# Moving the transfers of an S5 branch from SyncE's queue to GpSimd's

## The chip, the cores and the metric

The kernel runs on one core of a Trainium2 chip. The time is the device time of one execution in microseconds (us), as the median of several executions. The core has five engines that run their own instruction streams in order: TensorE (PE, with its weight loads shown as PEld), VectorE (DVE), ScalarE (ACT), GpSimd (POOL) and SyncE (SP). Any of the last three can issue DMA transfers, and all transfers are carried by the same 16 DMA engines. In this kernel SyncE issues nearly all of them.

## The reference

The model is a trunk of two layers on 272 tokens (16 meta tokens and 256 inputs) of width 2048, in float32. The first (even) layer is where the change lies. From one input projection it takes queries, keys and values for a grouped attention, and a stream u of width 512 for a bidirectional S5 branch: 32 groups of 16 channels, each with a diagonal complex state of 64, one recurrence per direction. Both results are joined, projected, and followed by a squared-ReLU MLP; the second (odd) layer and its MLP come after and are not touched.

```
def s5_direction(u, lam_re, lam_im, log_dt, b_re, b_im, c_re, c_im):
    ...                     # abar = exp(lam * dt), bbar = (abar - 1) / lam * b, complex
    bu_re = jnp.einsum('blgh,gph->blgp', u, bbar_re)
    bu_im = jnp.einsum('blgh,gph->blgp', u, bbar_im)
    ...
    _, _, x_re, x_im = lax.associative_scan(_complex_scan_combine, (a_re, a_im, bu_re, bu_im), axis=1)
    return jnp.einsum('blgp,ghp->blgh', x_re, c_re) - jnp.einsum('blgp,ghp->blgh', x_im, c_im)

def s5_mixer(u, ...):
    y_fw = s5_direction(uf, ...)
    y_bw = flip_t(s5_direction(flip_t(uf), ...))
    y = y_fw + y_bw + d_skip.astype(f32) * uf
    y = jax.nn.gelu(y.reshape(b, l, S5_WIDTH))
    return y * jax.nn.sigmoid(y @ glu_w.astype(f32) + glu_b.astype(f32))

def even_mixer(h, ...):
    q, k, v, u = jnp.split(h @ w_in, ...)
    ...
    att = grid_attention(q, k, v.reshape(b, l, ATT_KV_HEADS, HEAD_DIM))
    ssm = s5_mixer(u, ...)
    return jnp.concatenate([att.astype(jnp.float32), ssm], axis=-1).astype(h.dtype) @ w_out
```

## The kernel before

All large projections go through one helper, `stream` (from L140). It reads a weight matrix in chunks of mostly 512 KB: each chunk is loaded into a tile `raw` by a DMA on SyncE (L176), split by ScalarE into a rounded high half `wh` (L133) and by VectorE into the rest `wl` (L134), and used by TensorE in three matmuls per block (L166): high by high, high by low, low by high. `raw`, `wh` and `wl` have four buffers each, so a load waits until an older chunk has been split. The activations are split the same way into `xh` and `xl` (L136, L137).

The even layer runs two programs woven into one another in the text. The main one (`even_in`) streams the weights of u first, then ten chunks of q, k and v columns with the attention behind each group of heads, then (`out_a`) the first part of the output projection. The side program is the S5 branch (`S5.run`, then `S5.tail`). It doesn't scan token by token. Tokens are cut into 34 blocks of 8: matrices that hold powers of abar carry a block's inputs to its end state, a scan of 34 steps runs over the blocks, and more matrices bring the states back to the tokens. Groups are handled in eight batches of four:

- `evac_u` (L717) scales the projected u into a tile `up` and stores it to a scratch in DRAM, `s_u` (L724, 4 transfers); `finish_u` (L726) reads it back rearranged into the tile `U` (L731, 8 transfers; each has 16 partitions with 32 runs of 136 bytes). Clearing the edge of the state array EE, which lies in the buffer h, is a GpSimd operation (L927).
- `batch` (L810) loads the b and c coefficients of four groups, `bc` (L815), builds on VectorE the tables W and CA (L734 is the line of the helper through which all these tensor operations go), transposes W (L856) into WT, multiplies CA by bb (L867), stores CA to a DRAM scratch `s_ca` (L870), and assembles from the product a tile `Kf` of 16 partitions. Eight transfers (L880) copy shifted windows of Kf, four runs of 512 bytes in each of 16 partitions, into the 128 partitions of the matrix `M`. CA, Kf, M, W and WT have one buffer each, bc has two.
- `apply` (L885) multiplies WT and M by U (`pe`, L893, and `pm`, L902).
- After the last batch two transfers (L928, L929) swap the halves of EE (shown as h<-h), and the scan runs on VectorE (L931 on). `tail` reloads CA (L959), applies it (L963, L964), and moves the result through DRAM once more (L976, L978) before the gate `glu`.

GpSimd has little else in this layer: four loads of constants at the start, and clears of edge regions of `V`, `qr` and `sq` for the attention (L641, L578).

The order of the work on each engine is not written by hand. A planner goes through the program with a model of each engine's time, and takes what is ready by priority: the place in the text, moved ahead by 50 for the split and load of weights, by 500 for `URGENT` pieces such as `apply` and the scan, and by 0 for a batch's tables. Each engine then runs its list in order, and each wait at the head of a list holds what stands behind.

Of the kernel before, what the change touches and what calls it, by code (L numbers as in the profile page):

```python
# [15 lines left out]
P = 128  # L16
# [687 lines left out]
class S5:  # L704
# [12 lines left out]
    def evac_u(self, ft):  # L717
        nc = self.nc
        acc = self.T.h[:, ft]
        up = self.p2.tile([P, S5C, S5J], F32, name="up", tag="sg")  # L720
        nc.vector.tensor_tensor(out=up.rearrange("p s j -> p j s"),
                                in0=acc.rearrange("p (j s) -> p j s", s=S5C),
                                in1=self.T.rb.rearrange("p (j s) -> p j s", s=S5C), op=ALU.mult)
        nc.sync.dma_start(out=self.ud[ft * P:(ft + 1) * P], in_=up)  # L724

    def finish_u(self):  # L726
        nc = self.nc
        self.U = self.p1.tile([P, S5G, S5J], F32, name="U")
        v = self.ud.rearrange("(g h) s j -> s h g j", h=16)
        for s in range(S5C):  # L730
            nc.sync.dma_start(out=self.U[s * 16:(s + 1) * 16], in_=v[s])  # L731

    def tt(self, out, a, b, op):
        self.nc.vector.tensor_tensor(out=out, in0=a, in1=b, op=op)  # L734
# [75 lines left out]
    def batch(self, b):  # L810
        nc, I, p1, p2, tt, T = self.nc, self.I, self.p1, self.p2, self.tt, self.T
        mul, add, sub = ALU.mult, ALU.add, ALU.subtract
        g0 = b * NB
        bc = p2.tile([P, 4, 2, NB, 16], F32, name="bc")
        nc.sync.dma_start(out=bc, in_=I["s5_bc"][:, b])  # L815
        bb = p1.tile([P, 2, 2, NB, 16], F32, name="bb")
        nc.vector.tensor_scalar_mul(out=bc[:, 2:], in0=bc[:, 2:], scalar1=self.sg[:, 1:2])
        btmp = p1.tile([P, 2, NB, 16], F32, name="btmp")

        def gsel(x):  # L820
            return x.rearrange("p (d g) -> p d g", d=2)[:, :, g0:g0 + NB].unsqueeze(3).broadcast_to([P, 2, NB, 16])

        cr, ci = gsel(self.cr), gsel(self.ci)
        tt(bb[:, 0], bc[:, 0], cr, mul)
        tt(btmp, bc[:, 1], ci, mul)
        tt(bb[:, 0], bb[:, 0], btmp, add)
        tt(bb[:, 1], bc[:, 1], cr, mul)
        tt(btmp, bc[:, 0], ci, mul)
        tt(bb[:, 1], bb[:, 1], btmp, sub)
        yield  # L830

        def table(dst, tmp, Pa, Pb, A, B, d, lo, n, rev):
            ks = slice(lo, lo + n)

            def pw(x):
                v = x[:, ks, d * S5G + g0:d * S5G + g0 + NB]
                if rev:
                    v = v[:, ::-1]
                return v.rearrange("p k g -> p g k").unsqueeze(3).broadcast_to([P, NB, n, 16])

            def cf(x):
                return x.unsqueeze(2).broadcast_to([P, NB, n, 16])

            tt(dst, pw(Pa), cf(A), mul)
            tt(tmp, pw(Pb), cf(B), mul)
            tt(dst, dst, tmp, add)

        W = p1.tile([P, 2, NB, S5C, 16], F32, name="W")
        wt = p1.tile([P, NB, 9, 16], F32, name="wtmp")
        WT = p1.tile([P, 2, NB, P], F32, name="WT")  # L850
        for d in range(2):
            table(W[:, d], wt[:, :, :S5C], self.P1, self.P2, bb[:, 0, d], bb[:, 1, d], d, 0, S5C, d == 0)
            with T.tc.high_priority(offset=URGENT):
                pt = T.mx([P, NB, P], "wtp")
                for g in range(NB):
                    nc.tensor.transpose(pt[:, g], W[:, d, g].rearrange("p s h -> p (s h)"), T.ident)  # L856
                nc.scalar.copy(out=WT[:, d], in_=pt)
            yield
        CA = p1.tile([P, 2, NB, 9, 16], F32, name="CA")
        kp = []  # L860
        for d in range(2):
            table(CA[:, d], wt, self.P1, self.P2, bc[:, 2, d], bc[:, 3, d], d, 0, 9, d == 1)
            with T.tc.high_priority(offset=URGENT):
                ps = T.mx([16, NB, P], "kps")
                for g in range(NB):
                    lo = 0 if d == 0 else 1
                    nc.tensor.matmul(ps[:, g], bb[:, 0, d, g], CA[:, d, g, lo:lo + 8], start=True, stop=True)  # L867
            kp.append(ps.rearrange("p g (t h) -> p g t h", h=16))
            yield
        nc.sync.dma_start(out=self.cad[b], in_=CA.rearrange("p d g t h -> p (d g t h)"))  # L870
        Kf = p1.tile([16, NB, 15, 16], F32, name="Kf")
        nc.scalar.copy(out=Kf[:, :, 8:15], in_=kp[0][:, :, 1:8])
        nc.scalar.copy(out=Kf[:, :, 0:8], in_=kp[1])
        tt(Kf[:, :, 7], kp[0][:, :, 0], Kf[:, :, 7], add)
        dm = p1.tile([16, NB, 16], F32, name="dm")
        tt(dm, self.drow[:, g0:g0 + NB], T.ident[:16, :16].unsqueeze(1).broadcast_to([16, NB, 16]), mul)
        tt(Kf[:, :, 7], Kf[:, :, 7], dm, add)
        M = p1.tile([P, NB, P], F32, name="M")
        for s in range(S5C):
            nc.sync.dma_start(out=M[s * 16:(s + 1) * 16].rearrange("p g (t h) -> p g t h", h=16),  # L880
                                in_=Kf[:, :, 7 - s:15 - s])
        yield
        self.batches.append((b, WT, M))
# [22 lines left out]
    def run(self):  # L906
        nc, T, p1, p2, tt = self.nc, self.T, self.p1, self.p2, self.tt
        mul, add = ALU.mult, ALU.add
        self.batches = []
        yield from self.base()  # L910
        for b in range(S5G // NB):
            bt = self.batch(b)
            while True:
                with T.tc.high_priority(offset=0):
                    if next(bt, 0) == 0:
                        break
                yield
            while not hasattr(self, "U"):
                yield
            ap = self.apply(*self.batches.pop())  # L920
            while True:
                with T.tc.high_priority(offset=URGENT):
                    if next(ap, 0) == 0:
                        break
                yield
        EE = self.EE
        nc.gpsimd.memset(EE[:, :, 0], 0.0)  # L927
        nc.sync.dma_start(out=EE[64:, 1, 1:], in_=EE[:64, 0, 1:])  # L928
        nc.sync.dma_start(out=EE[:64, 1, 1:], in_=EE[64:, 0, 1:])  # L929
        yield  # L930
        for j in range(1, S5J - 1):  # L931
            with T.tc.high_priority(offset=URGENT):
                t1 = p2.tile([P, 2, 64], F32, name="z1")
                t2 = p2.tile([P, 2, 64], F32, name="z2")
                x = EE[:, :, j]
                tt(t1, self.PP[:, 0], x, mul)
                tt(t2, self.PP[:, 1], x[:, ::-1], mul)
                tt(t1, t1, EE[:, :, j + 1], add)
                tt(EE[:, :, j + 1], t1, t2, add)
            if j % 4 == 0:  # L940
                yield
# [454 lines left out]
```

## Time and profile before

| | us |
|---|---|
| median of three runs | 2409.11 (2406.84 to 2411.78) |
| profiled execution | 2411.23 |
| its span, first to last instruction | 2409.3 |
| TensorE busy | 2348.9 (97%) |
| VectorE busy | 1441.7 (60%) |
| ScalarE busy | 1132.0 (47%) |
| GpSimd busy | 64.4 (3%) |

Mean granted TensorE clock is 0.989 of full speed. A profile row gives the engine, the line of the kernel, the operation, the tile it writes and what it reads; `[2.59 <-DVE wl L134]` at the end of a row says that the engine was idle for 2.59 us just before, and which operation ended that. SPq is SyncE's queue, whose rows are the issues of transfers; when the data landed is told in a view of its own. A matmul's duration overlaps that of the next one, so the rate is read from counts, not durations.

### The profile page before, as it was taken

How to read it: one execution, taken by the hardware profiler on the slowest of the kernel's cores; microseconds unless marked ns; L12 is line 12 of the kernel's file. 1: busy time of each engine (PE TensorE's matmuls, PEld its weight loads, DVE VectorE, ACT ScalarE, POOL GpSimd, SP SyncE). 2: the span in 40 equal slices, each digit the busy share in tenths (PEclk: the TensorE clock that was granted, in tenths of full speed). 3: DMA queues.
4: the chain of work that ended last, by engine and by line, in shares of the span. 5: the costliest groups of instructions: out<-in, count | busy, mean ns of one | idle time of the engine just before them, and what ended most of it. 6: DMA issues, size and time to landing. Idle time of an engine off the chain costs nothing.

```text
span 2409.3 us, 42429 instructions
## 1 busy us (share of the span) xinstructions
PE 2348.9 (97%) x17287; PEld 2243.4 (93%) x17287; DVE 1441.7 (60%) x2351; ACT 1132.0 (47%) x1754; POOL 64.4 (3%) x116
## 2 busy tenths in 40 slices
PE   7999999999999999999989999999999999999998
PEld 7889899999999999999989999999988988988987
DVE  8786837654554454555679667656644544555555
ACT  5566734543443343344456434444544443443443
POOL 0000001100000000000110000001000000000000
PEclk9999999999999999999999999999999999999999
DMA  7545464555555555555452543564555555555554
GB/s 265 167 146 174 125 199 141 166 172 176 171 181 176 176 169 182 170 180 183 161 174 83 167 149 125 189 198 146 183 185 190 185 176 189 187 186 192 184 186 146
DMA packets 131458, 415.49 MB, mean 172 GB/s; under 512 B 23504, under 2 KB 30048, under 8 KB 130496
## 3 DMA queue, kind: packets, MB, share of 16 engines
q1 hardware_dynamic: 130816, 412.35, 53.7%
q8 instruction: 135, 2.21, 0.4%
q14 instruction: 59, 0.48, 0.1%
q0 software_dynamic: 160, 0.35, 0.1%
q10 hardware_dynamic: 288, 0.10, 0.0%
HBM read 401.62 MB, written 7.95 MB: 170 GB/s over the span
## 4 chain that ended last, share of the span: by engine, by line
PE 89%; DVE 4%; ACT 2%; POOL 1%; issue 1%; DMA 0%; DVEq 0%; SPq 0%; ACTq 0%; POOLq 0%
PE acc L166 81%; POOL h L293 1%; DVE wl L134 1%; PE po L690 1%; DVE res L290 1%; DVE xl L137 1%; PE mo L1180 1%; PE pe L893 1%; PE kps L867 1%; PE sc L667 1%; PE ro L1256 1%; ACT wh L133 0%; PE ptp L683 0%; PE pc L219 0%; PE rs L1247 0%
## 5 line engine op out<-in xcount | busy, mean ns | idle before, releaser
L134 DVE TENSOR_TENSOR wl<-raw,wh 128x1024 fp32r<-128x1024 f32 (+1 forms) x730 | 890.2, 1220 | 840.1 <-ACT wh L133 836.4
L133 ACT CAST wh<-raw 128x1024 fp32r<-128x1024 f32 (+1 forms) x730 | 757.9, 1039 | 1013.1 <-PE acc L166 968.1
L166 PE MATMUL acc<-xh,wh 128*128 128x272 f32 (+1 forms) x3728 | 1070.8, 288 | 25.4 <-ACT wh L133 9.7
L166 PE MATMUL acc<-xl,wh 128*128 128x272 f32 (+1 forms) x3728 | 1073.1, 288 | 5.5 <-DVE xl L137 5.1
L166 PE MATMUL acc<-xh,wl 128*128 128x272 f32 (+1 forms) x3728 | 1070.9, 288 | 6.5 <-DVE wl L134 6.5
L166 PEld LDWEIGHTS acc<-xh,wh 128*128 128x128 f32 x3728 | 707.3, 190 | 28.9 <-ACT wh L133 9.8
L166 PEld LDWEIGHTS acc<-xl,wh 128*128 128x128 f32 x3728 | 709.4, 190 | 9.2 <-DVE xl L137 7.8
L166 PEld LDWEIGHTS acc<-xh,wl 128*128 128x128 f32 x3728 | 707.6, 190 | 9.3 <-DVE wl L134 7.6
L166 PE MATMUL acc<-h1l,wh 128*128 128x272 f32 x1024 | 295.8, 289 | 0.0
L166 PE MATMUL acc<-h1h,wl 128*128 128x272 f32 x1024 | 295.2, 288 | 0.0
L166 PE MATMUL acc<-h1h,wh 128*128 128x272 f32 x1024 | 293.8, 287 | 0.0
L166 PE MATMUL acc<-wh,h1l 128*128 128x512 f32 (+1 forms) x528 | 204.8, 388 | 0.0
L166 PE MATMUL acc<-wh,h1h 128*128 128x512 f32 (+1 forms) x528 | 204.7, 388 | 0.0
L166 PE MATMUL acc<-wl,h1h 128*128 128x512 f32 (+1 forms) x528 | 203.9, 386 | 0.0
L166 PEld LDWEIGHTS acc<-h1h,wh 128*128 128x128 f32 x1024 | 193.0, 188 | 0.0
L166 PEld LDWEIGHTS acc<-h1l,wh 128*128 128x128 f32 x1024 | 192.7, 188 | 0.0
L166 PEld LDWEIGHTS acc<-h1h,wl 128*128 128x128 f32 x1024 | 192.4, 188 | 0.0
L166 PEld LDWEIGHTS acc<-wh,h1l 128*128 128x128 f32 x528 | 99.2, 188 | 21.8
L166 PEld LDWEIGHTS acc<-wl,h1h 128*128 128x128 f32 x528 | 99.3, 188 | 21.6
L166 PEld LDWEIGHTS acc<-wh,h1h 128*128 128x128 f32 x528 | 99.4, 188 | 21.1
L293 POOL TENSOR_TENSOR h<-h,res 128x272 f32<-128x272 f32 (+1 forms) x42 | 47.8, 1152 | 576.0 <-DVE res L290 576.0
L368 ACT ACTIVATE relu<-acc 128x272 f32<-128x272 f32 (+1 forms) x128 | 48.3, 391 | 27.5 <-PE acc L166 27.5
(319 smaller groups left out, 1492.9 us busy)
## 6 DMA issues: line engine op xcount, KB each, us to landing
raw<-in_w SPq DMA_DIRECT2D x504, 512.0 KB, 3.5
raw<-in_w_odd SPq DMA_DIRECT2D x88, 512.0 KB, 3.4
raw<-in_w_even SPq DMA_DIRECT2D x40, 512.0 KB, 4.4
raw<-in_wo_odd SPq DMA_DIRECT2D x24, 512.0 KB, 3.9
raw<-in_wo_a SPq DMA_DIRECT2D x24, 384.0 KB, 3.9
s_ca<-CA SPq DMA_DIRECT2D x8, 576.0 KB, 3.6
CA<-s_ca SPq DMA_DIRECT2D x8, 576.0 KB, 4.8
h<-in_hT SPq DMA_DIRECT2D x16, 272.0 KB, 4.5
```

What stands on the lines that cost most here:

```text
L133: nc.scalar.copy(out=hi, in_=src)
L134: nc.vector.tensor_tensor(out=lo, in0=src, in1=hi.bitcast(F32), op=ALU.subtract)
L137: nc.vector.scalar_tensor_tensor(out=lo, in0=src, scalar=scale, in1=hi.bitcast(F32), op0=ALU.mult, op1=ALU.subtract)
L166: nc.tensor.matmul(a, lt, rt, start=k == 0 and j == 0, stop=k == nk - 1 and j == 2)
L290: nc.vector.scalar_tensor_tensor(out=t[:, :N], in0=self.y[:, k, t0:], scalar=self.gain(l, i, k), in1=rb(k)[:, :N], op0=ALU.mult, op1=ALU.mult)
L293: eng.tensor_tensor(out=self.h[:, k, t0:], in0=self.h[:, k, t0:], in1=t[:, :N], op=ALU.add)
L368: nc.scalar.activation(out=t[:, :N], in_=acc, func=AF.Relu)
L667: nc.tensor.matmul(ps[:, :L], qf[:, i * P:i * P + P], cur["k", g], start=True, stop=True)
L690: nc.tensor.matmul(po[:, :R // 2], cur["v", g][:, j], PT[j][:, c0:c0 + R // 2], start=j == 0, stop=j == 2)
L867: nc.tensor.matmul(ps[:, g], bb[:, 0, d, g], CA[:, d, g, lo:lo + 8], start=True, stop=True)
L893: nc.tensor.matmul(pev[:, d, g], WT[:, d, g], U[:, g0 + g], start=True, stop=True)
L1180: nc.tensor.matmul(po[:, d, :HD + 1], e[:, t:t + P], V[:, st], start=j == 0, stop=j == len(keys) - 1)
```

## The change

In seven places of the S5 branch the engine that issues a transfer is changed from SyncE to GpSimd; shapes, order in the text and everything else stay. The transfers of `tail` (its variable `dq` is `nc.sync`) and the weight loads stay on SyncE.

```
     def evac_u(self, ft):
...
-        nc.sync.dma_start(out=self.ud[ft * P:(ft + 1) * P], in_=up)
+        nc.gpsimd.dma_start(out=self.ud[ft * P:(ft + 1) * P], in_=up)
     def finish_u(self):
...
         for s in range(S5C):
-            nc.sync.dma_start(out=self.U[s * 16:(s + 1) * 16], in_=v[s])
+            nc.gpsimd.dma_start(out=self.U[s * 16:(s + 1) * 16], in_=v[s])
     def batch(self, b):
...
-        nc.sync.dma_start(out=bc, in_=I["s5_bc"][:, b])
+        nc.gpsimd.dma_start(out=bc, in_=I["s5_bc"][:, b])
...
-        nc.sync.dma_start(out=self.cad[b], in_=CA.rearrange("p d g t h -> p (d g t h)"))
+        nc.gpsimd.dma_start(out=self.cad[b], in_=CA.rearrange("p d g t h -> p (d g t h)"))
...
         for s in range(S5C):
-            nc.sync.dma_start(out=M[s * 16:(s + 1) * 16].rearrange("p g (t h) -> p g t h", h=16),
+            nc.gpsimd.dma_start(out=M[s * 16:(s + 1) * 16].rearrange("p g (t h) -> p g t h", h=16),
                                 in_=Kf[:, :, 7 - s:15 - s])
     def run(self):
...
-        nc.sync.dma_start(out=EE[64:, 1, 1:], in_=EE[:64, 0, 1:])
-        nc.sync.dma_start(out=EE[:64, 1, 1:], in_=EE[64:, 0, 1:])
+        nc.gpsimd.dma_start(out=EE[64:, 1, 1:], in_=EE[:64, 0, 1:])
+        nc.gpsimd.dma_start(out=EE[:64, 1, 1:], in_=EE[64:, 0, 1:])
```

## Rows read from the trace of the kernel before

**Rows 1.** The page, part 1: busy time, share of the span, instructions of an engine.

```profile
PE 2348.9 (97%) x17287; PEld 2243.4 (93%) x17287; DVE 1441.7 (60%) x2351; ACT 1132.0 (47%) x1754; POOL 64.4 (3%) x116
```

**Rows 2.** Windows: stretch, length, busy time (instructions) by engine, PEclk, DMA share, GB/s.

```profile
10.00:45.00 35.00, 30.86 (x215) 28.82 (x214) 34.59 (x91) 27.24 (x41) 0.00 (x0) 1.00 0.85 305
45.00:90.00 45.00, 41.52 (x316) 39.61 (x315) 29.49 (x61) 17.93 (x35) 0.21 (x1) 0.96 0.62 159
90.00:350.00 260.00, 257.67 (x1878) 236.05 (x1877) 180.97 (x468) 157.43 (x318) 1.25 (x7) 0.98 0.53 162
450.00:500.00 50.00, 50.00 (x403) 50.00 (x402) 26.10 (x35) 22.27 (x33) 0.00 (x0) 1.00 0.53 173
```

**Rows 3.** Waits of TensorE, 45 to 350 us: total, times, longest.

```profile
PE acc L166 <- DVE wl L134: 3.2, 2, 2.6
```

**Rows 4.** Waits of SyncE's queue, 0 to 350 us.

```profile
SPq L176 <- DVE wl L134: 74.5, 36, 7.0
...
SPq L880 <- DVE Kf L734: 27.1, 8, 5.7
SPq L870 <- DVE CA L734: 15.9, 5, 9.8
```

**Rows 5.** Timeline of SyncE's queue: start, length, issue, count; merged issues stand together.

```profile
42.65 6.43 SPq L880 DMA_DIRECT2D M<-Kf  x8
...
56.90 5.03 SPq L731 DMA_DIRECT2D U<-s_u  x8
71.76 0.34 SPq L870 DMA_DIRECT2D s_ca<-CA  x1
72.22 0.35 SPq L176 DMA_DIRECT2D raw<-in_w_even  x1
72.62 0.92 SPq L815 DMA_DIRECT2D bc<-in_s_bc  x1
```

**Rows 6.** Timeline of TensorE, 56 to 86 us.

```profile
71.12 0.52 PE L166 MATMUL acc<-xh,wl 128*128 128x272 f32 x2 [2.59 <-DVE wl L134]
...
73.73 1.87 PE L893 MATMUL pe<-U,WT 128*128 128x34 f32 x16
...
79.39 0.39 PE L166 MATMUL acc<-xh,wh 128*128 128x272 f32 x1 [0.26 <-ACT wh L133]
...
80.79 0.52 PE L166 MATMUL acc<-xh,wl 128*128 128x272 f32 x2 [0.64 <-DVE wl L134]
```

**Rows 7.** Timeline of VectorE, 69 to 80 us.

```profile
69.85 1.22 DVE L134 TENSOR_TENSOR wl<-raw,wh 128x1024 fp32r<-128x1024 f32 x1
...
78.80 0.35 DVE L817 TENSOR_SCALAR bc<-bc,sgn 128x256 f32<-128x256 f32 x1 [7.07 <-DMA bc<-in_s_bc]
```

**Rows 8.** Timeline of ScalarE, near 64 and near 162 us.

```profile
64.42 1.05 ACT L133 CAST wh<-raw 128x1024 fp32r<-128x1024 f32 x1
...
162.14 0.39 ACT L644 COPY V<-vt 128x256 f32<-128x256 f32 x1
```

**Rows 9.** Line 880 alone: ns of one issue (least, median, most), first and last start.

```profile
L880 SPq DMA_DIRECT2D M<-Kf x64: 585/593/1776, 42.6 to 225.4; - x64
```

**Rows 10.** Timeline of GpSimd, 0 to 350 us.

```profile
1.94 0.54 POOL L525 DMA_DIRECT2D cosE<-in_rope_even  x1
...
139.04 0.21 POOL L641 MEMSET V<- 128x128 f32 x1 [8.32 <-PE po L690]
```

**Rows 11.** Transfers of the whole kernel: count, KB of one, median us to landing.

```profile
bc<-in_s_bc SPq DMA_DIRECT2D x8, 256.0 KB, 3.8
...
U<-s_u SPq DMA_DIRECT2D x8, 68.0 KB, 4.9
...
cosE<-in_rope_even POOLq DMA_DIRECT2D x1, 136.0 KB, 5.7
```

**Rows 12.** One window near the end of the S5 branch, columns as in rows 2.

```profile
305.00:310.00 5.00, 5.00 (x27) 5.00 (x27) 0.96 (x1) 0.83 (x1) 0.00 (x0) 0.57 0.44 154
```

## The prediction

> **What bounds the kernel now.** I read the page first, then the windows, then the waits, and only then single instructions. TensorE is busy for 97% of the span, GpSimd for 3% [rows 1], so time is won or lost only where TensorE stands idle or runs slowly. All the work that the change touches lies in the even layer's first 350 us. The windows [rows 2] cut these into the start (10 to 45 us), the first weight streams after it (45 to 90) and the rest (90 to 350); the fourth window is a stretch of pure streaming, 403 matmuls in 50 us, which gives 0.124 us from one matmul to the next. Idle time is the window less TensorE's busy time: 45.00 - 41.52 = 3.5 us from 45 to 90 us, 260.00 - 257.67 = 2.3 us from 90 to 350. After 45 us the change can thus win back at most 5.8 us of idle time, 0.24% of the span. At the start I count matmuls, since a waiting one can be counted as busy: 215 x 0.124 = 26.7 us of work in 35 us, 8.3 us lost. VectorE is busy there for 34.59 of 35.00 us, so it is VectorE that paces the start, not a queue.
>
> The waits of TensorE name the largest piece after that: 3.2 us on wl, the low half of the split weights, 2.6 of it in one wait [rows 3]. The waits of SyncE's queue show what the change removes: beside its own kind of wait (L176, 74.5 us, for a weight buffer that VectorE frees) stand 27.1 us at L880 (the M transfers wait for Kf) and 15.9 us at L870 (s_ca waits for CA) [rows 4]. In those times every weight load behind in the same queue is held up, whether it could start or not. SyncE's timeline shows the two worst places [rows 5]: eight M transfers hold the queue from 42.65 to 49.08 us, and after the U loads, which end at 56.90 + 5.03 = 61.93 us, nothing is issued until CA is ready at 71.76 us; a weight load and a load of bc follow at once, at 72.22 and 72.62.
>
> **What did that blocking cost?** Less than the waits suggest. The 2.6 us stall ends at 71.12 us, when wl is there [rows 6]. That wl ran on VectorE at 69.85 us [rows 7], although the cast that feeds it had ended on ScalarE at 64.42 + 1.05 = 65.47 us [rows 8]: it stood in VectorE's order behind the CA tables. Its weights had landed before the cast, so the queue was not what it waited for, and with the same order on VectorE the stall stays. VectorE then sat idle for 7.07 us until bc had landed [rows 7]. That one is the queue's doing, but TensorE had work until 79 us, and pays for it with 0.26 us and 0.64 us [rows 6].
>
> **Part by part.** 94 transfers move: 4 of s_u, 8 of U, 8 of bc, 8 of s_ca, 64 of M, 2 of EE. The tail's own transfers (CA reloads, s_y, gT) stay on SyncE, so the words "all transfers" go further than the edit does.
>
> (1) *SyncE without the S5 waits.* The blocked weight loads can start up to 71.76 - 61.93 = 9.8 us sooner. What of that ends on TensorE's path lies between 0 and all the idle time of that window, -3.5 us. I take the two short waits alone, 0.26 + 0.64 = -0.9 us, because only their chain runs through SyncE.
>
> (2) *M on GpSimd.* One M transfer holds SyncE for 0.593 us [rows 9]. The nearest row on GpSimd is the load of cosE, 0.54 us for 128 rows [rows 10]; an M transfer has 16 partitions with four runs each, 64 runs. Eight of them take 8 x 0.54 = 4.3 us, or half of that if the runs set the price, against 8 x 0.593 = 4.7 us. M is issued no later: 0 us. Queued behind M on GpSimd are only the next s_ca and bc and the clears of V, qr and sq (5).
>
> (3) *s_u and U.* U has a dated end: the matmuls pe read it first, at 73.73 us [rows 6]. Now the last U load is issued by 61.93 and lands 4.9 us later [rows 11], at 66.8 us, with 6.9 us to spare. On GpSimd the eight issues cost from 8 x 0.54 = 4.3 us (as cosE) to four times that, 17.3 us, if the price goes by runs: a U load has 16 x 32 = 512 runs, cosE 128. That lands U at 56.90 + 4.3 + 4.9 = 66.1 us or at 56.90 + 17.3 + 4.9 = 79.1 us. The stall begins when one issue costs over (73.73 - 4.9 - 56.90) / 8 = 1.49 us. I take 0 us, since even the middle of the bounds (1.35 us) keeps the date; the upper end, 79.1 - 73.73 = +5.4 us, is a rival.
>
> (4) *bc, s_ca, EE.* Single issues, about 0.54 us on GpSimd against 0.92 for the bc at 72.62 us on SyncE [rows 5]. The first bc would stand behind GpSimd's four loads of the start and could go out before some of the first weights: 256 KB in front of them, at the 305 GB/s that the queues move there [rows 2], is up to +0.9 us, and nothing if it lands in a gap. I take 0, because VectorE paces the start.
>
> (5) *Clears on GpSimd.* They now share a queue with transfers that wait. The clear of V at 139.04 us [rows 10] is needed by the copy into V at 162.14 us [rows 8], 23 us later. The longest thing ahead of it would be a wait of 5.7 us for Kf [rows 4] and eight issues of 0.54, together 10 us. 0 us.
>
> (6) *Order.* The planner that orders every engine's program counts each issue on the engine that makes it. With 94 of them moved, the splits, tables and S5 matmuls can fall into another order, which no row of before shows. Its bounds: at best the 5.8 us of idle time go. At worst another stall of 2.6 us comes up and another dip of the clock like that at 305 to 310 us, where the granted clock was 0.57, near the lower of its two levels (1.2 and 2.4 GHz), and 27 matmuls were begun [rows 12] where 40 fit: 13 x 0.124 = 1.6 us. Together +4.2 us. I take 0, between ends of opposite sign.
>
> Sum: -0.9 + 0 + 0 + 0 + 0 + 0 = -0.9 us. The profiled execution took 2411.23 us, 1.9 us more than its span of 2409.3, and lies 2.1 us above the median of the three runs. On that median the sum gives 2409.1 - 0.9 = 2408.2 us.
>
> On the landing: GpSimd's cosE landed after 5.7 us, SyncE's loads of bc after 3.8 [rows 11], but the first in the crowded start. The Trainium skill, "DMA: Bandwidth & Descriptors", section "Latency and other measured facts", gives about 1 us to the first byte from GpSimd and 0.6 from SyncE; an estimate from it is 0.4 us more for each dependent transfer, by which the sum would be -0.5 us and U would still be in time. No like transfers stand under one load here, so the trace can't decide it.
>
> **Rivals.** *A, faster:* the planner sees weights arrive on time and puts their splits ahead of the tables, and the stalls go. For it: the two longest holds of SyncE lie at or in the window with most idle time [rows 2, 5]. Against it: the largest stall's chain runs through VectorE. Price: -5.8 us if all idle time after 45 us goes, 2403.3; if half of the 8.3 us lost at the start goes too, because the first batch's tables move behind the splits, -10.0, 2399.1.
>
> *B, slower:* GpSimd builds U's many short runs one by one and takes over 1.49 us an issue; pe then stands at the head of TensorE's queue and everything behind it waits. Price at the upper bound +5.4 us, 2414.5; with a dip of the clock after that gap (1.6 us) 2416.1. For it: U has four times the runs of any transfer that GpSimd makes now. Against it: the 6.9 us, and that the planner can put pe later.
>
> *C, slower:* on VectorE the splits fall behind S5's tables more often than now, since the tables of several batches become ready at once when bc no longer waits in SyncE's queue. For it: one such place already costs 2.6 us [rows 6, 7]. Against it: the splits have the higher priority. One more stall and dip, +4.2 us, still lies in the band; two of each, +8.4 us, give 2417.5.
>
> *D, it does nothing:* SyncE's S5 waits fall and L176 takes them over, since a weight load also needs a buffer that VectorE frees, by far the longest wait there now [rows 4]. That gives 2409.1 and falls in with the forecast. The Trainium skill, "DMA: Bandwidth & Descriptors", section "Issuing engines are not separate DMA queues", holds that several issuing engines save the sequencer's time alone; by it D would be the whole story.
>
> **How the numbers follow.** A measurement of this kernel can tell about 0.2% (4.8 us) from no change; the three runs lie 4.9 us apart. The band is 2404.3 to 2413.9. Forecast and D: 0.44. A: 0.28. B: 0.15, C from its second stall on: 0.13. So faster 0.28, same 0.44, slower 0.28. The range of 8 in 10 goes from A's far end, 2399.1, to C's 2417.5, each widened by the half spread of the runs, 2.5: 2397 to 2420.
>
> **What would show it.** Right: SyncE's waits at L880 and L870 are gone, on GpSimd an issue of M takes about 0.54 us and one of U under 1.49, U lands before the first pe, and TensorE's idle time from 45 to 350 us stays within 3 us of 5.8. Wrong: a wait of pe for U, a copy into V that waits for a clear on GpSimd, another count of matmuls at the start, or a time outside the band.

## The result and the profile after

The changed kernel takes 2437.14 us (median of 4 runs, 2434.79 to 2439.62) against 2407.98 us of the kernel before: ratio 1.0114, 95% interval 1.0099 to 1.0129. It is slower by 1.1%, some 27 us by the ratio and 29 us by the medians, and lies above the range on record. The profiled execution took 2436.37 us with a span of 2434.6, so the spans differ by 2434.6 - 2409.3 = 25.3 us. Executions of the kernel before lie up to 10 us apart (2405.66 to 2415.55 in one set of 16), so a difference of a few us between two profiled executions says little by itself.

Where do the 25.3 us arise? Two marks in time divide the span. The first is the last evacuation on line 515, with which the even layer's output product ends; the second is the first of the closing instructions on line 1391, the kernel's last line. The rows are a line's instructions: count, ns of one (least, median, most), first and last start. First the kernel before:

```profile
L515 DVE TENSOR_TENSOR y<-acc,part x4: 431/432/433, 393.0 to 398.6; 128x272 f32<-128x272 f32 x4
L1391 SPq EVENT_SEMAPHORE  x9: 17/28/1792, 2406.3 to 2409.2; - x9
L1391 POOLq DRAIN  x3: 40/102/2189, 2403.5 to 2409.0; - x3
```

The same rows of the changed kernel:

```profile
L515 DVE TENSOR_TENSOR y<-acc,part x4: 428/431/433, 413.7 to 419.3; 128x272 f32<-128x272 f32 x4
L1391 SPq EVENT_SEMAPHORE  x11: 17/28/28, 2426.7 to 2434.5; - x11
L1391 POOLq DRAIN  x3: 46/102/9868, 2423.9 to 2434.3; - x3
```

The even layer ends at 419.3 instead of 398.6 us, +20.7. Between the marks nothing changes much: the closing begins 2426.7 - 2406.3 = 20.4 us later. The closing itself lasts 7.8 us instead of 2.9, +4.9. GpSimd's longest DRAIN there takes 9.87 us instead of 2.19; what it waits for no run shows.

In the even layer the windows of the changed kernel say what TensorE lost (columns as in rows 2; the first three stretches are those of [rows 2]):

```profile
10.00:45.00 35.00, 28.67 (x202) 26.29 (x201) 33.76 (x92) 25.71 (x38) 2.30 (x5) 1.00 0.86 307
45.00:90.00 45.00, 44.63 (x343) 44.11 (x342) 31.32 (x48) 22.41 (x36) 11.43 (x21) 0.96 0.76 231
90.00:350.00 260.00, 246.72 (x1751) 223.24 (x1751) 174.79 (x467) 149.17 (x307) 36.49 (x75) 0.94 0.45 134
...
90.00:250.00 160.00, 158.95 (x1193) 144.31 (x1192) 117.27 (x252) 97.30 (x194) 35.27 (x72) 0.99 0.46 142
250.00:300.00 50.00, 38.33 (x214) 32.08 (x214) 30.78 (x128) 29.26 (x67) 1.22 (x3) 0.83 0.32 76
...
250.00:260.00 10.00, 0.95 (x6) 0.94 (x5) 0.00 (x0) 0.00 (x0) 1.05 (x2) 0.74 0.90 178
260.00:270.00 10.00, 10.00 (x44) 9.07 (x44) 5.01 (x26) 6.23 (x16) 0.17 (x1) 0.58 0.10 28
```

At the start 13 fewer matmuls are begun than before. From 45 to 90 us the change did what its description suggests: idle time fell from 3.5 to 0.4 us and 27 more matmuls were begun. From 90 to 350 us the idle time rose from 2.3 to 13.3 us, the granted clock fell from 0.98 to 0.94, and 127 fewer matmuls were begun, 15.7 us at 0.124. Nearly all of that lies in one place. Up to 250 us the changed kernel is ahead by 27 + 12 - 13 = 26 matmuls; from 250 to 300 us it begins 214, and the kernel before 339:

```profile
90.00:250.00 160.00, 158.80 (x1181) 144.11 (x1180) 119.02 (x278) 105.22 (x213) 1.25 (x7) 0.99 0.52 163
250.00:300.00 50.00, 48.87 (x339) 43.20 (x338) 46.21 (x164) 36.91 (x81) 0.00 (x0) 1.00 0.41 123
...
260.00:270.00 10.00, 10.00 (x85) 9.98 (x84) 8.51 (x32) 6.64 (x15) 0.00 (x0) 1.00 0.30 87
```

From 250 to 260 us TensorE begins 6 matmuls, and VectorE and ScalarE do nothing at all. In the next 10 us TensorE looks busy, but its granted clock is 0.58 and it begins 44 matmuls, where 85 are begun before.

The waits of TensorE (45 to 440 us) and of SyncE's queue (0 to 350 us) in the changed kernel: total, times, longest.

```profile
PE pm L902 <- DMA M<-Kf: 9.1, 1, 9.1
...
PE acc L166 <- ACT wh L133: 1.4, 1, 1.4
...
SPq L176 <- DVE wl L134: 158.7, 43, 21.1
```

SyncE's waits at L880 and L870 [rows 4] are gone, and the wait of weight loads for a buffer, 74.5 us before, is now 158.7 us: SyncE waits no less than it did, for another thing. TensorE has one new wait, 9.1 us for the last batch of M. GpSimd's timeline shows where that comes from:

```profile
43.78 4.08 POOL L880 DMA_DIRECT2D M<-Kf  x8 [3.76 <-ACT rc L251]
...
59.98 5.02 POOL L731 DMA_DIRECT2D U<-s_u  x8 [2.19 <-DMA s_u<-up]
...
242.91 0.54 POOL L928 DMA_DIRECT2D h<-h  x1 [7.91 <-DMA gw<-in_glu_w]
243.75 3.59 POOL L880 DMA_DIRECT2D M<-Kf  x7 [0.30 <-issue]
255.60 0.51 POOL L880 DMA_DIRECT2D M<-Kf  x1 [8.26 <-DMA h<-h]
```

The planner put the first swap (L928) ahead of the last eight M. In this program GpSimd's transfers take turns on eight semaphores, so each waits until the eighth before it has landed; the eighth M after the swap, which neither reads nor writes h, therefore stood 8.26 us until the swap had landed, and pm stood behind that M. That is the gap from 250 to 260 us.

How far the order moved can be counted in the two programs: ahead of the first pe stand 360 of the stream's matmuls (line 166) before and 492 after, ahead of the last pe 948 and 1106, ahead of line 985 1519 and 1551. Step (6), taken at zero, is thus no small matter, and it is this new order that puts the swap ahead of the last M.

### The profile page after: what moved, and what is told of

Read it like the earlier page. It is cut to its first block, busy times and chain, and to the rows that moved or that the text cites. A ratio compares the mean times of both kernels' runs of the same rounds, so it can differ in the third digit from the quotient of the medians.

```text
span 2434.6 us, 42471 instructions
## 1 busy us (share of the span) xinstructions
PE 2357.2 (97%) x17287; PEld 2249.4 (92%) x17287; DVE 1445.5 (59%) x2351; ACT 1133.2 (47%) x1754; POOL 114.0 (5%) x210
## 4 chain that ended last, share of the span: by engine, by line
PE 87%; DVE 4%; ACT 3%; issue 2%; DMA 2%; POOL 1%; SPq 0%; DVEq 0%; ACTq 0%; POOLq 0%
PE acc L166 79%; POOL h L293 1%; DVE wl L134 1%; DVE xl L137 1%; DVE res L290 1%; PE po L690 1%; PE mo L1180 1%; ACT wh L133 1%; DMA h<-h 1%; PE ro L1256 1%; PE kps L867 0%; PE pe L893 0%; PE py L964 0%; PE py L963 0%; ACT pe L672 0%
```

## The experiments

All times below are medians of an experiment and of the kernel before on the same chip, and "the even layer's end" is the last start on line 515 in the profiled execution, against 398.6 us of before. No experiment leaves out a part of the computation. In the first eight expectations A is the theory that the new places of the branch's steps in the planned order cost the time, B that GpSimd's queue and landings do, and C, from the fifth on, that transfers from GpSimd are dear in themselves (not the prediction's rival C); each says what its rivals give.

**One part undone or done alone.** The first four runs put the swaps back on SyncE, put s_u and U back, move only s_u and U, and move only the swaps:

```diff
 e1 (on the changed kernel)
-        nc.gpsimd.dma_start(out=EE[64:, 1, 1:], in_=EE[:64, 0, 1:])
-        nc.gpsimd.dma_start(out=EE[:64, 1, 1:], in_=EE[64:, 0, 1:])
+        nc.sync.dma_start(out=EE[64:, 1, 1:], in_=EE[:64, 0, 1:])
+        nc.sync.dma_start(out=EE[:64, 1, 1:], in_=EE[64:, 0, 1:])
 e4 (on the kernel before): the same two lines the other way
 e2 (on the changed kernel)
-        nc.gpsimd.dma_start(out=self.ud[ft * P:(ft + 1) * P], in_=up)
+        nc.sync.dma_start(out=self.ud[ft * P:(ft + 1) * P], in_=up)
-            nc.gpsimd.dma_start(out=self.U[s * 16:(s + 1) * 16], in_=v[s])
+            nc.sync.dma_start(out=self.U[s * 16:(s + 1) * 16], in_=v[s])
 e3 (on the kernel before): the same two lines the other way
```

> The changed kernel with the two EE swaps (L928, L929) back on SyncE; all else stays on GpSimd. In its program the last batch's pe still stands behind 1106 stream matmuls, as in the changed kernel, against 948 in the kernel before. Theory A (the S5 branch falls behind the weight stream, so less stream work is left to cover its scan and tail): the 158 matmuls x 0.124 us = 19.6 us of cover stay lost, 15 to 25 us over the kernel before. Theory B (the EE swap on GpSimd's queue lands late and the last M transfer waits for it): 0 to +4 us over the kernel before. Both acting in a row: +8 to +15 us.

Measured: 2431.33 against 2409.63 us, ratio 1.0084 (1.0064 to 1.0103); the even layer's end 413.9 (+15.3), the wait of pm 2.4 instead of 9.1 us. That fits A, and the swap's place in GpSimd's queue seemed to be worth the other 5.4 us.

> The changed kernel with s_u and U back on SyncE. In its program the last batch's pe stands behind 1019 stream matmuls (948 before, 1106 changed). Theory A: (1019 - 948) x 0.124 = +8.8 us over the kernel before. Theory B: the EE swap still shares GpSimd's queue with the last M, so nearly all of the loss stays, +25. Both in a row: +15 to +21 us.

Measured: 2431.16 us, ratio 1.0083 (1.0063 to 1.0102); the even layer's end 409.9 (+11.3). By the ratio that is +20 us, what A and B together give, and far more than A's 8.8 alone.

> The kernel before with only s_u and U moved to GpSimd. In its program the last batch's pe stands behind 1048 stream matmuls (948 before). Theory A: (1048 - 948) x 0.124 = +12.4 us. Theory B: 0 us, since the EE swaps and M stay on SyncE.

Measured: 2428.09 us, ratio 1.0069 (1.0049 to 1.009); the even layer's end 414.1 (+15.5).

> The kernel before with only the two EE swaps moved to GpSimd. Its program has the stream and S5 in the order of the kernel before up to the swap (948 matmuls before the last pe). Theory A: 0 us. Theory B in the form 'GpSimd's swap lands later': up to 12.4 - 4.5 = +8 us at the start of the scan, of which what the stream doesn't cover; in the form 'M waits for the swap's landing in the same queue': 0 us, as M is on SyncE.

Measured: 2414.04 us, ratio 1.001 (0.9998 to 1.0023); the even layer's end 401.1 (+2.5). The first pe, last pe and last pm have the places of the kernel before here (360, 948 and 1022 matmuls ahead), and the loss is small.

U back and U alone cannot both be explained by U: each costs more than half of the whole. The parts do not add up, +15.3, +11.3, +15.5 and +2.5 us. That speaks against a price per transfer, and for plans that differ as wholes.

**Place of the steps, with and without GpSimd.** Two knobs of the kernel shift the branch in the planned order without any transfer moved: SIDE_EVEN, how fast the branch is woven into the stream, and the priority of a batch.

```diff
 e5 (on the changed kernel) and e7 (on the kernel before)
-SIDE_EVEN = 1.6
+SIDE_EVEN = 2.2
 e6 (on the kernel before)
-                with T.tc.high_priority(offset=0):
+                with T.tc.high_priority(offset=-150):
                     if next(bt, 0) == 0:
```

> The changed kernel with the S5 branch woven more densely into the stream (SIDE_EVEN 2.2 for 1.6), so that the last batch's pe stands behind 960 stream matmuls (948 before, 1106 changed); all 94 transfers stay on GpSimd, and the last M still waits for the EE swap's landing. Theory A (place of the S5 branch in the stream): (960 - 948) x 0.124 = +1.5 us over the kernel before, and with the swap's part of 5 to 9 us left +6 to +10. Rival C (transfers from GpSimd are dear in themselves, the place doesn't matter): +25 us as in the changed kernel.

Measured: 2446.1 against 2410.51 us, ratio 1.0149 (1.0134 to 1.0164); the even layer's end 428.9 (+30.3). Far from A, and above C's +25 too. TensorE now waits 21.9 us for M, more than twice as long as in the changed kernel. Its waits, and two windows:

```profile
PE pm L902 <- DMA M<-Kf: 21.9, 2, 13.9
...
130.00:180.00 50.00, 40.90 (x259) 35.56 (x258) 30.48 (x75) 25.17 (x58) 10.90 (x23) 0.83 0.28 91
220.00:260.00 40.00, 25.62 (x143) 22.20 (x144) 16.89 (x72) 18.73 (x46) 6.08 (x13) 0.74 0.49 129
```

> The kernel before, every transfer on SyncE, with the priority of the S5 batches lowered by 150 places, so that the last batch's pe stands behind 1062 stream matmuls (948 before). Theory A: (1062 - 948) x 0.124 = +14.1 us with no transfer on GpSimd at all. Rival C: 0 us.

Measured: 2425.8 us, ratio 1.0059 (1.0039 to 1.0079), the even layer's end 417.8 (+19.2), with every transfer on SyncE. A is met by the ratio (+14.2 us), and C, which expected nothing, falls.

> The kernel before with SIDE_EVEN 2.2 for 1.6: the last batch's pe stands behind 885 stream matmuls (948 before), all transfers on SyncE. Theory A, if the kernel before still lacks cover for scan and tail: up to (885 - 948) x 0.124 = -7.8 us; if its cover is already enough: 0 us. Rival C says nothing else than 0 us.

Measured: 2425.6 us, ratio 1.0064 (1.0049 to 1.0079), the even layer's end 414.9 (+16.3), again with every transfer on SyncE. Here A expected a gain. So later steps lose and earlier steps lose as well: the place alone, in the form that A gave it, does not set the time. C expected nothing here either.

```diff
 e8 (on the kernel before)
-            nc.sync.dma_start(out=M[s * 16:(s + 1) * 16].rearrange("p g (t h) -> p g t h", h=16),
+            nc.gpsimd.dma_start(out=M[s * 16:(s + 1) * 16].rearrange("p g (t h) -> p g t h", h=16),
```

> The kernel before with only the 64 M transfers moved to GpSimd, two thirds of all that move. In its program the last batch's pe stands behind 950 stream matmuls (948 before). Theory A: 0 us (within 3). Rival C: the loss goes by the number of transfers, 64 of 94 of 27 us, +18 us.

Measured: 2423.24 us, ratio 1.0058 (1.0035 to 1.0081); the even layer's end 410.8 (+12.2). A expected nothing, C +18.

After eight runs A had failed three times (e5, e7, e8), C twice (e6, e7), and in every run that moved a transfer the order had changed with it. The next two take them apart.

**Order and queue taken apart.** Both kernels trace the same instructions in the same sequence of program text, 94 of them with another engine. So one kernel's planned order can be forced on the other: an ordering edge from each instruction to the next one of its engine, without a semaphore.

```diff
         Trunk(tc, I, out).build()
+        hold_order(nc, tc)
...
+def hold_order(nc, tc):
+    ins = list(nc.cur_bb.bb.instructions)
+    for chain in json.loads(zlib.decompress(base64.b85decode("".join(ORDER)))):
+        for p, q in zip(chain, chain[1:]):
+            tc.add_manual_dep(ins[q], ins[p].name,
+                              mybir.DependencyInfo(mybir.DependencyClass.NoSync, mybir.DependencyReason.DATA),
+                              reason="hold_order")
```

ORDER holds one list of positions in the program text for each engine. TensorE, VectorE, ScalarE, GpSimd's computing instructions, SyncE's other transfers and the 94 among themselves then stand exactly as in the kernel whose order is taken. How the 94 and the other transfers share SyncE's queue, where both are on it, is left to the planner.

> All 94 transfers on GpSimd as in the changed kernel, and TensorE, VectorE, ScalarE, SyncE's other transfers and the 94 among themselves issue in exactly the order of the kernel before (ordering edges, no semaphores). Theory P (the loss is in the new order of the instructions): the even layer ends within 0 to +4 us of before's 398.6 (the swaps and M stand in the order of before, and their landings are 1 to 2 us longer on GpSimd); the closing stretch on line 1391 is 7.8 us against 2.9, as in the changed kernel: together +5 to +9 us, ratio 1.002 to 1.004. Rival Q (GpSimd's queue and its longer landings hold TensorE up): the even layer ends 15 to 21 us late as in the changed kernel, +20 to +27 us, ratio 1.008 to 1.011. Rival R (the closing stretch is longer because the order is, not because transfers were moved): closing stretch 2.9 us.

Measured: 2415.08 against 2409.86 us, ratio 1.0023 (1.0012 to 1.0034). The even layer's end and the closing instructions (line 1503 here):

```profile
L515 DVE TENSOR_TENSOR y<-acc,part x4: 431/432/434, 392.3 to 397.9; 128x272 f32<-128x272 f32 x4
L1503 SPq EVENT_SEMAPHORE  x11: 17/28/28, 2404.3 to 2412.2; - x11
L1503 POOLq DRAIN  x3: 46/98/9868, 2401.6 to 2412.0; - x3
```

With all 94 transfers on GpSimd and the order of before, the even layer ends 0.7 us earlier than before, which is less than two executions differ by. The closing lasts 2412.2 - 2404.3 = 7.9 us, as in the changed kernel. Q falls, P holds, and R falls with it: the closing follows the transfers, not the order.

> All 94 transfers on SyncE as before, and every engine issues in exactly the order of the changed kernel (the 94 among themselves too, so the first swap stands ahead of the last batch of M). Theory P: the even layer ends 15.3 to 20.7 us late (the lower end is the run with the swaps alone on SyncE, the upper the changed kernel itself), the closing stretch is 2.9 us: +15 to +21 us, ratio 1.006 to 1.009. Rival Q: 0 to +3 us in all, ratio 1.000 to 1.001. What the changed kernel's even layer ends later than this one is the price of GpSimd's queue at the same order: 0 to 5.4 us.

Measured: 2432.2 against 2409.86 us, ratio 1.0096 (1.0082 to 1.0109).

```profile
L515 DVE TENSOR_TENSOR y<-acc,part x4: 431/432/434, 413.7 to 419.3; 128x272 f32<-128x272 f32 x4
L1506 SPq EVENT_SEMAPHORE  x9: 17/28/1787, 2426.8 to 2429.7; - x9
```

With no transfer moved and the order of the changed kernel, the even layer ends at 419.3 us, the same tenth as in the changed kernel, and the closing lasts 2.9 us as before. Q falls: the new order loses as much without GpSimd's queue. That the ends are equal is luck, however, for the time goes in other places. TensorE runs the same sequence in this run and in the changed kernel, and another in the kernel before and in e9; the matmuls begun are:

| us | 10 to 45 | 45 to 90 | 90 to 250 | 250 to 300 | 300 to 350 | 350 to 400 |
|---|---|---|---|---|---|---|
| before | 215 | 316 | 1181 | 339 | 362 | 387 |
| e9: order of before, all on GpSimd | 212 | 328 | 1181 | 350 | 348 | 381 |
| changed kernel | 202 | 343 | 1193 | 214 | 347 | 349 |
| e10: order of the changed kernel, none on GpSimd | 146 | 332 | 1195 | 295 | 374 | 305 |

Against the kernel before, e10 loses 69 matmuls at the start, 44 from 250 to 300 us and 82 from 350 to 400 us; the changed kernel loses 13, 125 and 38 there. The rows behind it are, for e10, VectorE's wait up to 45 us, TensorE's waits from 10 to 425 us, and the first and last start of pe and pm:

```profile
DVE bc L817 <- DMA bc<-in_s_bc: 10.3, 2, 5.4
...
PE acc L166 <- ACT wh L133: 5.5, 1, 5.5
...
PE pm L902 <- DMA M<-Kf: 1.4, 1, 1.4
...
L893 PE MATMUL pe<-U,WT x128: 193/278/298, 97.0 to 249.4; 128*128 128x34 f32 x128
L902 PE MATMUL pm<-U,M x64: 192/277/278, 98.7 to 259.9; 128*128 128x34 f32 x64
```

and for the changed kernel:

```profile
DVE bc L817 <- DMA bc<-in_s_bc: 3.5, 1, 3.5
...
L893 PE MATMUL pe<-U,WT x128: 192/278/298, 89.4 to 241.7; 128*128 128x34 f32 x128
L902 PE MATMUL pm<-U,M x64: 192/277/407, 91.1 to 260.6; 128*128 128x34 f32 x64
```

The new order wants bc early on VectorE; on SyncE it stands among the weight loads, and VectorE waits 10.3 us for it instead of 3.5. So e10's last pe is 7.7 us behind that of the changed kernel (249.4 and 241.7 us). Its last pm is 0.7 us ahead (259.9 and 260.6): between the two the changed kernel loses 8.4 us more, nearly all of it the wait behind the swap. The first run fits that: with the swaps on SyncE pm waits 2.4 us, and 280 matmuls are begun from 250 to 300 us. In e9, GpSimd's queue with the order of before, it waits 0.5 us. So that wait belongs to the order and GpSimd's queue together, and neither alone makes it.

What the order costs is therefore read from kernels that differ in nothing else: with all 94 on GpSimd 419.3 - 397.9 = 21.4 us at the even layer's end (the changed kernel and e9), with none 419.3 - 398.6 = 20.7 us (e10 and the kernel before). The move with the order of before costs nothing in the even layer and some 5 us in the closing.

**What in the order costs?** VectorE's share looked telling. Two rows for line 134 from 240 to 300 us, first before, then after: 15 splits of weights against 6.

```profile
L134 DVE TENSOR_TENSOR wl<-raw,wh x15: 947/952/1220, 243.4 to 298.0; 128x768 fp32r<-128x768 f32 x13, 128x1024 fp32r<-128x1024 f32 x2
```

```profile
L134 DVE TENSOR_TENSOR wl<-raw,wh x6: 949/952/959, 245.6 to 298.5; 128x768 fp32r<-128x768 f32 x6
```

In the traces the longest run of VectorE instructions that reaches into the scan and holds no split of weights is 27 before, 41 in the run with the swaps alone, 68 after and 63 to 103 in the other runs that lost 11 us or more (the expectation below gives partly other counts). Theory G made that the cause. It can be tried in both directions, with all else of VectorE's order held and the other engines planned around it:

```diff
 e11 (on the kernel before): places of the splits of line 134 in VectorE's order
-421 448 450 477 487
+421 484 485 486 487
 e12 (on the changed kernel): places of the splits of line 134 in VectorE's order
-406 475 492 499 530 538 550
+406 429 452 475 498 518 550
```

> The kernel before, all transfers on SyncE, VectorE's order held, but three of its 14 splits of stream weights among the scan's instructions (the wl of line 134 that stand 448th, 450th and 477th on VectorE) stand next to the one at 487, so that 62 of VectorE's instructions run without a split where 27 did. ScalarE and TensorE are planned around it and change in nothing before the last relevant stretch; the steps of S5 before the scan stand where they did. Theory G (the price of an order is the longest stretch of the scan in which VectorE makes no split: 28 instructions in before, 42 in the run with the swaps alone that lost 2.5 us, 55 to 77 in those that lost 11 to 21): the even layer ends 10 to 16 us late, ratio 1.004 to 1.007. Rival H (the place of S5's earlier steps among the stream's matmuls is what counts, the splits have 4 buffers and are ahead): 0 to +3 us, ratio 1.000 to 1.001.

Measured: 2412.24 against 2410.78 us, ratio 1.0004 (0.9994 to 1.0013); the even layer's end 399.8 (+1.2). H holds.

> The changed kernel, all 94 transfers on GpSimd and its own order on VectorE, but five splits of stream weights (wl of line 134, standing 475th, 492nd, 499th, 530th and 538th) are moved ahead into the scan, so that its longest stretch without a split is 32 instructions instead of 69. The place of S5's steps up to the last batch stays that of the changed kernel (492 stream matmuls ahead of the first, 1106 ahead of the last). Theory G: most of the 20.7 us at the even layer's end comes back, 0 to 8 us of it stay (a stretch of 52 earlier on VectorE and the wait for M remain), and the 4.9 us at the end stay: +5 to +13 us, ratio 1.002 to 1.005. Rival H: nothing comes back, +23 to +27 us, ratio 1.010 to 1.011.

Measured: 2446.1 us, ratio 1.0143 (1.0128 to 1.0158); the even layer's end 429.5 (+30.9). Worse than the changed kernel, where G expected most of the loss back. The first py starts at 327.1 instead of 321.0 us: with the five splits moved into it the scan ends later. H's ratio, at most 1.011, is missed too. G falls twice; that splits and losses went together in ten programs was no cause.

The last two try cover, with all else of TensorE's order held: the branch's last products (line 985, glu) stand 50 of the stream's matmuls earlier in the good order, later in the bad one.

```diff
 e13 (on the kernel before): matmuls of line 166 ahead of line 985 in TensorE's order
-1519
+1469
 e14 (on the changed kernel): matmuls of line 166 ahead of line 985 in TensorE's order
-1551
+1602
```

> The kernel before, all transfers on SyncE, TensorE's order held but for one thing: the branch's last 16 products (line 985) stand 50 of the stream's matmuls earlier (1469 ahead of them instead of 1519), so that 150 instead of 200 stand between the first py and them. Theory V (cover: the branch's steps from py to line 985 last 41 to 47 us in every run, whatever stands in between, and TensorE idles for what its order lacks there): 50 matmuls of 0.124 us, 6.2 us; the even layer ends +4 to +7 us late, ratio 1.0015 to 1.003. Rival W (these positions do not count; something else in the orders does, as in the run with the splits late): 0 to +1.5 us, ratio within 0.0007.

Measured: 2421.91 against 2411.28 us, ratio 1.0045 (1.0032 to 1.0057); the even layer's end 411.5 (+12.9). Of that, 5.0 us were there before the edited place: the first py starts at 303.1 instead of 298.1 us, since in this execution the granted clock was 0.74 from 60 to 80 us and 0.84 from 80 to 100, where the program is still that of before. From py to the even layer's end it is 411.5 - 303.1 = 108.4 us against 398.6 - 298.1 = 100.5, +7.9. What TensorE waits for at line 985, and the window of it:

```profile
  DMA gT<-s_y: 7.2, 1
...
340.00:360.00 20.00, 14.80 (x75) 12.91 (x76) 8.32 (x15) 6.35 (x13) 0.00 (x0) 0.83 0.50 176
```

The chain from py to gT does not get shorter when less work stands beside it: gT arrives at its own time, TensorE waits 7.2 us, and the granted clock of the window is 0.83. V has the sign and the place, and 7.9 us instead of 6.2; its ratio, at most 1.003, is exceeded, and how much of that is the early dip of the clock is known for the profiled execution alone.

> The changed kernel, all 94 transfers on GpSimd and its own order on TensorE, but the branch's last 16 products (line 985) stand 50 of the stream's matmuls later (about 1600 ahead of them instead of 1551). Theory V: the 4.9 us that this kernel loses on before between the first py and line 985 (44.3 us with 175 stream matmuls against 42.5 us with 200) come back: even layer's end +15 to +17.5 us instead of +20.7, in all +20 to +22.5, ratio 1.008 to 1.0095. Rival W: +20 to +21 at the even layer's end, ratio 1.010 to 1.011.

Measured: 2439.2 us, ratio 1.0111 (1.0096 to 1.0127); the even layer's end 423.6 (+25.0), in the slowest of four executions. V falls here: the wait for gT is gone, but nothing comes back, since 50 more matmuls stand in a stretch in which their weights are not ready. By the ratio it is neither better nor worse than the changed kernel (1.0114), which is W.

```profile
PE acc L166 <- ACT wh L133: 3.7, 2, 3.3
...
360.00:380.00 20.00, 16.09 (x85) 14.13 (x84) 8.27 (x11) 7.85 (x13) 0.00 (x0) 0.83 0.83 255
```

So the good order has cover up to the branch's last products, and taking it away costs (e13); the bad order can't be mended at that one place. Of what the order costs, the runs place 8.4 us: the swap ahead of the last M, with all of it on GpSimd. What setting the swap alone behind the last M would give back at the end was not tried; in the first run, where the wait is 2.4 us, the even layer ends 5.4 us earlier. Which traits account for the rest stays open.

**The closing.** It needs no run of its own, since GpSimd's longest DRAIN goes with the number of its transfers in all of them. The rows of the runs with the swaps alone, with U and s_u alone and with M alone:

```profile
L1391 POOLq DRAIN  x3: 40/102/2351, 2406.3 to 2411.5; - x3
...
L1391 POOLq DRAIN  x3: 46/102/3172, 2419.4 to 2424.8; - x3
...
L1391 POOLq DRAIN  x3: 46/102/7420, 2413.8 to 2421.8; - x3
```

With 0 of the 94 moved it is 2.19 us, with 2 2.35, with 12 3.17, with 64 7.42 and with 94 9.87: about 0.08 us for each transfer, though the changed kernel issued the last of them at 256.1 us. e1 and e2, with 92 and 82, lie on the same line (9.71 and 8.89 us). The DRAIN begins 2.8 us ahead of the closing (2403.5 and 2406.3 us before, 2423.9 and 2426.7 after), so a short one does not lengthen the closing and a long one does: it lasts 2.9, 2.7, 3.0, 5.4 and 7.8 us.

## Why the prediction was wrong

The predicted 2408.2 us was missed by 29 us, and the sign with it.

*Steps (1) to (5)* held with the order of before. All 94 transfers on GpSimd then end the even layer 0.7 us earlier (e9); the sum of the steps was -0.9, and that the two lie so close is luck, given how far executions differ. An issue of M takes 0.51 us on GpSimd (4.08 / 8; 0.54 expected), one of U 5.02 / 8 = 0.63, far below the 1.49 from which rival B decides, although it has 512 runs: B falls. U was issued by 65.0 and lands 6.1 us later in the median, long before the first pe, now at 89.4 us. No copy into V waits for a clear. Landings became longer in the changed kernel, with U 6.1 instead of 4.9 us and bc 5.4 instead of 3.8 [rows 11]; with the order of before they are 4.1 and 4.6 (e9).

*Step (6)* is the one that failed. It put the price of a new order between -5.8 and +4.2 us and took 0. It measured +21.4 us at the even layer's end with all 94 transfers on GpSimd (the changed kernel against e9) and +20.7 us with none (e10). The bound was worked out from the small stalls of the kernel before, one stall of 2.6 us and one dip of 1.6; but those stalls are small because this order leaves so little idle. They say what could be won, and nothing about how bad a neighbouring order can be. Of the eight other plans in which nothing was held (e1 to e8), two of them without a moved transfer, seven lost 11 us or more; the eighth, e4, keeps the order of before up to the last pm.

*Step (2)* fails with it. "M is issued no later: 0 us" reckoned with s_ca, bc and clears in M's new queue, and not with the swap; in the new order the last M is issued 8.26 us late behind the swap, and pm waits 9.1 us for it.

*Rival C* had the right sign and the right cause one level up, the order, but at +8.4 us less than half of the size. Its mechanism, splits behind tables, is not what the changed kernel shows: TensorE's waits for wl from 45 to 350 us, 3.2 us before [rows 3], are not longer there but gone. *Rival A*'s premise came true, weights came sooner and the idle time from 45 to 90 us fell by 3.1 us; the 26 matmuls that the changed kernel is ahead at 250 us are lost behind it. *Rival D* also came true, in that L176 took over SyncE's waits (74.5 to 158.7 us, and 173.8 in e9); with the order held it was the whole story in the even layer.

*The end of the kernel* was no step at all: +4.9 us, one fifth of the 25.3, in a stretch 2000 us behind the last line that the change touches.

The Trainium skill, "DMA: Bandwidth & Descriptors", section "Issuing engines are not separate DMA queues", holds that several issuing engines save the sequencer's time alone. With the order held e9 agrees for the even layer (-0.7 us); for the whole kernel it does not hold here, since the closing grows by 4.9 us.

The forecast of what would show it was useful in part: the idle time from 45 to 350 us, 0.4 + 13.3 = 13.7 us instead of 5.8 within 3, was the row that pointed to the order. One of its signs of being wrong came true at the start, 202 matmuls instead of 215, but 13 x 0.124 = 1.6 us is little of the loss.

## What to carry to other kernels

Where a planner orders the engines' programs, moving an issue to another engine is two changes, the transfer and the plan, and the second can be far larger; compare the two orders first, and hold the old one while you measure the move. Compare stretch by stretch and not the end alone: two kernels ended their even layer at the same tenth and had lost the time in different places. Do not bound the price of another order by the stalls of a good one. And look at the last microseconds: here the transfers on GpSimd, landed long before, were paid for in the kernel's closing.

## What the runs showed of the hardware

- GpSimd's price of an issue hardly depends on the number of short runs: 0.51 us for M with 64 runs, 0.54 for cosE with 128 [rows 10], 0.63 for U with 512.
- GpSimd's closing DRAIN grows by about 0.08 us with each transfer that it issued in the whole kernel: 2.19 us with none of the 94, 9.87 with all, in either order of the rest (e9), though the last was issued more than 2000 us earlier.
- Windows in and behind which TensorE stood idle show a granted clock between its two levels (1.2 and 2.4 GHz, 0.5 and 1 of full speed): in the changed kernel 0.74 in the 10 us with the wait of 9.1 us and 0.58 in the next 10, 0.83 with e13's wait of 7.2 us, 0.74 in e5's window with 14.4 of 40 us idle. The 50 matmuls that e13 took away are 6.2 us; it lost 7.9.
- Two programs that differ in 94 transfers' engines, but not in the order of the rest, end their even layer within 0.7 us of each other in one order and in the same tenth in the other, in the second by losses in different places.
